# One 512-column matmul over high and low activations per high weight tile in the first MLP product, with four PSUM banks a group

## The chip, the core and the metric

The kernel runs on one core of a Trainium2 chip. Its time is device time in microseconds (us), the median over executions. A core has a matrix engine (TensorE, called PE in the profile, with the loading of its stationary operand listed as PEld), a vector engine (VectorE, DVE), an activation engine (ScalarE, ACT), GpSimd (POOL) and a queue for transfers from and to HBM (SP). PE writes its products into PSUM, eight banks of 128 partitions by 512 fp32 values. DVE and ACT read PSUM and SBUF; each engine runs its own instructions in a fixed order and waits for the others by semaphores.

## What is computed

Two layers of a post-norm trunk over 256 tokens of 2048 channels. The part of a layer that the change touches is the MLP, a product with 2048x8192 weights, a squared ReLU, and a product back:

```python
    mix = jnp.concatenate([attn, h], axis=-1) @ w_out
    x = layer_norm(ALPHA * x + mix, ln1_g, ln1_b)

    f = jnp.square(jax.nn.relu(x @ w1)) @ w2
    return layer_norm(ALPHA * x + f, ln2_g, ln2_b)
```

Ahead of the MLP stand an input projection, attention over 8 heads, a depthwise convolution and an output projection.

## The kernel before

**Products.** Everything is fp32 and has to keep most of that precision. Each operand of a large product is held as two parts in a matmul format (type fp32r in the rows): a high part, rounded, and a low part, the remainder. A product is three passes: high weights by high activations, high weights by low activations, low weights by high activations, all summed in PSUM. The activations after a LayerNorm lie as tiles `xTa` (channels on partitions, columns 0 to 255 the high part of 256 tokens, columns 256 to 511 the low part).

**Weights.** They come in chunks of 1 MB (128 partitions by 2048 columns), in the order of use that `chunk_order` (L165) lists. `load_next` (L206) issues the transfer on SP; `cutting` (L220) rounds the chunk to `wh` on ACT (L236) and subtracts it to `wl` on DVE (L237, recorded as L86 like all that goes through the counting helper), each in two pieces. `get` keeps three chunks cut ahead of use. All chunks, raw or cut, and the squared activations `h` lie in 20 slots of SBUF, handed out first in, first out (`big`, `drop`, L130).

**The MLP of a layer.** The 8192 hidden channels are 16 groups of 512. Group 0 (`mlp_first`, L1018) has the activations stationary, since it starts while the LayerNorm still hands over tiles. Groups 1 to 15 (`mlp_in`, L1038) have the weights stationary: for each of the 4 chunks `kc` of a group, each of its 4 row blocks `ki` and each of 4 column blocks `m`, `stat_w` (L294) issues three matmuls of 256 columns, high by high, high by low, low by high, into the same half of a bank; two banks hold a group. That is 30 calls in both layers, 30 x 64 = 1920 triples, 5760 matmuls. At a group's end, per bank: ACT makes the ReLU from PSUM (`rl`, L1051), DVE multiplies PSUM's positive part by it (`sq`), ACT rounds that into `h` (L143), DVE subtracts for the low part. After groups 1 to 3 the second product (`w2`, tiles `w` in the rows) takes four groups at a time, with 512-column matmuls: in(4), product 0, in(5) to in(7), in(8), product 1 and so on; the last product goes through `close` (L653), which also starts the next LayerNorm.

**PSUM.** Four banks (tag `mm`, L115) serve the products, three (`ax`) the turning of tiles and small results, one (`cv0`) the convolution.

**Order.** The order of instructions on each engine comes from a scheduler that simulates a timeline of the whole program; it isn't written out by hand. A change in one part can move neighbours elsewhere.

Of the kernel before, what the change touches and what calls it, by code (L numbers as in the profile page):

```python
# [8 lines left out]
F32 = mybir.dt.float32  # L9
# [28 lines left out]
LEAD = 3.0  # L38
# chunks of weights whose low parts GpSimd computes: columns u by (group, rows), output projection by (columns, rows)
POOL_U = ((2, 3), (3, 0))  # L40
POOL_O = ((0, 0), (0, 1), (1, 0), (1, 1), (2, 0), (2, 1), (3, 1))
POOL_LO = {("u", 0, 0, kc) for kc in range(4)} | {("u", l, i, kc) for l in range(L) for i, kc in POOL_U} | {
    ("wo", l, 0, n, kc) for l in range(L) for n, kc in POOL_O}
# tiles (tokens, channels) of the input that VectorE gives their gain and offset
GV = ((1, 0), (1, 1), (0, 2))
# [24 lines left out]
def hybrid_trunk(ctx: ExitStack, tc: tile.TileContext, x, positions, inv_freq, ln_in_g, ln_in_b,  # L70
# [5 lines left out]
    class Counted:  # L76
        """an engine whose instructions add their rough cost to the clock, for the order in which work is issued."""
        def __init__(self, eng, key, cost):
# [32 lines left out]
    sm = ctx.enter_context(tc.tile_pool(name="sm", bufs=4))  # L111
    pp = ctx.enter_context(tc.tile_pool(name="pp", bufs=4, space=bass.MemoryType.PSUM))

# [1 line left out]
    def psum(name):  # L115
        return pp.tile([P, 512], F32, name=name, tag="mm", bufs=4)

    def psumx(name):
        return pp.tile([P, 512], F32, name=name, tag="ax", bufs=3)

    def psumc(name):
        return pp.tile([P, 512], F32, name=name, tag="cv0", bufs=1)

# [20 lines left out]

# [1 line left out]
    def rows(w, k0, nk):  # L146
# [122 lines left out]

# [1 line left out]
    vconv = []  # L271
# [20 lines left out]

# [1 line left out]
    def stat_w(ps, hi, lo, ki, ncol, act, first, last):  # L294
        """ps[m//2][:, m%2] += W[:, m]^T act, the weights stationary; act holds hi | lo."""
        for m in range(ncol // P):
            o = v3(ps[m // 2], 2)[:, m % 2]
            c = slice(m * P, (m + 1) * P)
            tensor.matmul(o, lhsT=hi[:, ki, c], rhs=act[:, 0:S], start=first and m % 2 == 0, stop=False,
                             skip_group_check=True)  # L300
            tensor.matmul(o, lhsT=hi[:, ki, c], rhs=act[:, S:2 * S], start=False, stop=False,
                             skip_group_check=True)
            tensor.matmul(o, lhsT=lo[:, ki, c], rhs=act[:, 0:S], start=False, stop=last,
                             skip_group_check=True)

    def stat_x(o, hi, lo, ki, act, t, first, last):
        """o += act[:, t]^T W, the activations stationary."""
        xh = act[:, t * P:(t + 1) * P]
        xl = act[:, S + t * P:S + (t + 1) * P]
        tensor.matmul(o, lhsT=xh, rhs=hi[:, ki], start=first, stop=False)  # L310
        tensor.matmul(o, lhsT=xh, rhs=lo[:, ki], start=False, stop=False)
        tensor.matmul(o, lhsT=xl, rhs=hi[:, ki], start=False, stop=last)

# [1 line left out]
    X = cst.tile([P, 2, D], F32, name="X")  # L315
# [80 lines left out]
    def after_norm(N, keys, ps, lag):  # L396
        """the first product after a LayerNorm, activations stationary: token tile 0 leads by lag chunks."""
        def mm(t, kc):
# [34 lines left out]

# [1 line left out]
    class First(Norm):  # L435
        """the input's LayerNorm: gain and offset per partition after the turn, over the free axis later."""
        def nrm(self, t, n, eng=None):
# [80 lines left out]
    def prepare():  # L518
        """small parameters with channels on partitions; rope tables with tokens on partitions."""
        wdr = big("wdr")  # L520
# [53 lines left out]
    def rope(dst, src, t, nh, name):  # L574
        """dst (P, nh, 64) SBUF from src (P, nh, 64) PSUM."""
        c = cosT[:, t].unsqueeze(1).unsqueeze(1).broadcast_to([P, nh, 2, 32])
        s = sinT[:, t].unsqueeze(1).unsqueeze(1).broadcast_to([P, nh, 2, 32])
        s4 = src.rearrange("p h (a c) -> p h a c", a=2)
        d4 = dst.rearrange("p h (a c) -> p h a c", a=2)
        a = work(f"ra{name}", "rp", 2).rearrange("p (h a c) -> p h a c", a=2, c=32)[:, :nh]  # L580
        b = work(f"rb{name}", "rp", 2).rearrange("p (h a c) -> p h a c", a=2, c=32)[:, :nh]
        vector.tensor_tensor(out=a, in0=s4, in1=c, op=ALU.mult)
        vector.tensor_tensor(out=b, in0=s4, in1=s, op=ALU.mult)
        vector.tensor_tensor(out=d4[:, :, 0], in0=a[:, :, 0], in1=b[:, :, 1], op=ALU.subtract)
        vector.tensor_tensor(out=d4[:, :, 1], in0=a[:, :, 1], in1=b[:, :, 0], op=ALU.add)

    def convolve(l, i, h, ca):
        """taps of the depthwise convolution for two channel tiles, one a step."""
        acc = [psumc(f"cv{l}{i}0")[:, :S], work(f"cv{l}{i}1", "cva1", 1, S)]
# [18 lines left out]
    def out_part(ps, tag, l, k0, n, kc, act, last):  # L608
        """PSUM of both token tiles += act^T W over chunk kc of the rows from k0, columns of chunk n."""
        hi, lo = get(tag, l, k0, n, kc)  # L610
# [7 lines left out]
    def out_tail(ps, tag, l, k0, n, act, tail, between):  # L618
        """the same for the last chunks, token tile 0 first."""
        nch = len(act)  # L620
# [32 lines left out]
    def close(tag, l, k0, act, N, first=False):  # L653
        """the last addition to X over all column chunks, the LayerNorm starting with token tile 0."""
        def between(i, ps):
# [19 lines left out]
    for l in range(L):  # L675
        hg = v3(big(f"hg{l}"), 8)
        ca = v3(big(f"ca{l}"), 8)

# [1 line left out]
        if l == 0:  # L680
# [25 lines left out]

# [1 line left out]
        gqb = work(f"gq{l}", "gb", 2)  # L708
# [46 lines left out]
        nc.gpsimd.memset(qrk[:, 1024:1024 + 2 * S], 0.0)  # L755
# [1 line left out]
        def u_group(i):  # L757
# [18 lines left out]

# [1 line left out]
        state.update(ahead=2, cap=5)  # L778
# [24 lines left out]

# [1 line left out]
        qn = v3(big(f"qn{l}"), H)  # L805
# [66 lines left out]

# [1 line left out]
        mixT = []  # L874
# [68 lines left out]

# [1 line left out]

        def cuts_after(i0, i1, ins):
            """the chunks of the output projection's second half from i0 are cut after these instructions."""
            first = index["wo", l, 8, 0, 0]
            for i in range(first + i0, first + i1):
                cut_after[i] = ins  # L950
# [39 lines left out]

# [1 line left out]
        ps2 = [out_banks("wo", l, 0, n) for n in range(2)]  # L992
# [21 lines left out]

# [1 line left out]
        hT = {}  # L1016
# [21 lines left out]
        def mlp_in(g):  # L1038
            ps = [psum(f"f{l}{g}{j}") for j in range(2)]
            for kc in range(4):  # L1040
                hi, lo = get("w1", l, g, kc)
                for ki in range(4):
                    stat_w(ps, hi, lo, ki, 512, N.xT[kc][:, ki], kc == 0 and ki == 0, kc == 3 and ki == 3)
                    if ki == 3:
                        retire("w1", l, g, kc)
                    tick()
            h = v3(big(f"h{l}_{g}", F32R), 4)
            hT[g] = h
            for j in range(2):
                r = work(f"rl{l}{g}{j}", "ev", 4)  # L1050
                nc.scalar.activation(r, ps[j], AF.Relu)  # L1051
                q = work(f"sq{l}{g}{j}", "ev", 4)
                vector.scalar_tensor_tensor(out=q, in0=ps[j], scalar=0.0, in1=r, op0=ALU.max, op1=ALU.mult)
                split(h[:, 2 * j:2 * j + 2, 0:S], h[:, 2 * j:2 * j + 2, S:2 * S], v3(q, 2))

        mlp_first(0)
        for g in range(1, QG):
            mlp_in(g)
        for q in range(NG // QG):
# [10 lines left out]
            else:  # L1070
                N.release()
                N = Norm(f"b{l}", ln2_g[l], ln2_b[l], last=l == L - 1)
                N.load()
                close("w2", l, q * 16, act, N)
                drop(*[f"h{l}_{q * QG + i}" for i in range(QG)])
# [34 lines left out]
```

## Time and profile before

| | |
|---|---|
| time, median of 3 runs (lowest to highest) | 2090.47 us (2089.58 to 2090.71) |
| span of the profiled execution | 2086.6 us |
| PE busy in it | 2013.5 us (97%), 12438 matmuls |
| DVE busy | 1316.8 us (63%), 1706 instructions |
| ACT busy | 896.8 us (43%), 1175 instructions |
| POOL busy | 211.4 us (10%) |
| mean granted clock of TensorE | 0.988 |

The span goes from the first to the last instruction. The two layers follow each other: layer 0's MLP lies between about 328 and 1055 us of the span, layer 1's between about 1346 and 2075. A busy share is a mean over stages with different limits, so the rows further down are by stage. In names such as f<-xTa,wh the tile before the arrow is written, the others are read.

### The profile page before, as it was taken

What the parts mean: (1) busy time and instruction counts of PE and PEld (TensorE: products, weight loads), DVE (VectorE), ACT (ScalarE), POOL (GpSimd) and SP (SyncE); (2) the same over time, 40 slices, a digit from 0 to 9 for tenths busy, and PEclk for the clock granted to TensorE, in tenths of its full rate; (3) what the DMA queues carried; (4) which work ended last, traced back from release to release, by engine and by line L of the source; (5) the groups of instructions that cost most, each with busy time, mean ns of one, the idle gap of its engine ahead of it and who ended that gap; (6) DMA issues with size and microseconds to landing.
All of it is one profiled execution on the core that took longest, in us unless ns stands there. A gap on an engine that the chain in (4) does not pass through costs nothing. (4 is left out here: it accounts for less than half of the span.)

```text
span 2086.6 us, 29734 instructions
## 1 busy us (share of the span) xinstructions
PE 2013.5 (97%) x12438; PEld 1815.8 (87%) x12438; DVE 1316.8 (63%) x1706; ACT 896.8 (43%) x1175; POOL 211.4 (10%) x152
## 2 busy tenths in 40 slices
PE   6899899999999999999999988999999999999997
PEld 5798787998998899899879987789889989988986
DVE  5999987545555545455569998865455455545455
ACT  5445464443443434344345544553334434434341
POOL 6412312000000000000020133110000000000001
PEclk9899999999999999999999999999999999999999
DMA  8465264545645655566546535544565456456561
GB/s 252 135 189 171 101 242 149 194 163 201 214 151 195 208 162 188 196 222 210 173 164 177 156 124 201 179 163 162 183 221 182 162 199 212 154 191 212 189 227 68
DMA packets 225317, 377.89 MB, mean 181 GB/s; under 512 B 15858, under 2 KB 69986, under 8 KB 223904
## 3 DMA queue, kind: packets, MB, share of 16 engines
q1 hardware_dynamic: 225120, 375.99, 54.1%
q8 instruction: 97, 1.59, 0.3%
q14 instruction: 36, 0.29, 0.0%
q10 hardware_dynamic: 64, 0.02, 0.0%
HBM read 373.88 MB, written 2.10 MB: 180 GB/s over the span
## 5 line engine op out<-in xcount | busy, mean ns | idle before, releaser
L86 DVE TENSOR_TENSOR wl<-wr,wh 128x1024 fp32r<-128x1024 f32 (+1 forms) x648 | 771.3, 1229 | 566.7 <-ACT wh L236 337.7
L236 ACT CAST wh<-wr 128x1024 fp32r<-128x1024 f32 (+2 forms) x700 | 685.7, 1031 | 809.8 <-DVE wl L86 353.1
L86 PE MATMUL f<-xTa,wh 128*128 128x256 f32 x3840 | 692.5, 283 | 0.0
L86 PE MATMUL w<-wh,h 128*128 128x512 f32 x2048 | 631.9, 389 | 0.0
L86 PEld LDWEIGHTS f<-xTa,wh 128*128 128x128 f32 x3840 | 599.4, 192 | 0.7
L86 PE MATMUL f<-xTa,wl 128*128 128x256 f32 x1920 | 542.8, 283 | 3.3 <-DVE wl L86 3.3
L86 PEld LDWEIGHTS w<-wh,h 128*128 128x128 f32 x2048 | 384.4, 188 | 79.7
L86 PE MATMUL w<-wl,h 128*128 128x512 f32 x1024 | 398.4, 389 | 0.0
L86 PEld LDWEIGHTS f<-xTa,wl 128*128 128x128 f32 x1920 | 368.2, 192 | 3.8 <-DVE wl L86 3.7
L86 DVE SCALAR_TENSOR_TENSOR cv<-hg,wdT,cv 128x255 f32<-128x255 f32 (+21 forms) x480 | 248.8, 576 | 4.3 <-ACT cv L592 4.1
L86 PEld LDWEIGHTS w<-wl,h 128*128 128x128 f32 x1024 | 192.2, 188 | 39.6
L323 POOL TENSOR_TENSOR rb<-vb,mhalf 128x1 f32<-128x1 f32 x4 | 4.2, 1047 | 1413.1 <-DVE nmub L86 1413.1
L237 POOL TENSOR_TENSOR wl<-wr,wh 128x1024 fp32r<-128x1024 f32 (+1 forms) x52 | 114.0, 2217 | 224.2 <-ACT wh L236 110.9
L86 PE MATMUL wo<-wh,mx 128*128 128x512 f32 x256 | 88.3, 421 | 11.8 <-DVE mx L86 10.9
L86 PE MATMUL wo<-wh,mc 128*128 128x512 f32 x256 | 79.9, 391 | 0.0
L86 DVE TENSOR_TENSOR X<-X,w 128x512 f32<-128x512 f32 x48 | 32.8, 687 | 72.7 <-PE w L86 72.6
L86 PE MATMUL u<-xTi,wh 128*128 128x256 f32 x384 | 73.8, 293 | 0.0
L86 PE MATMUL u<-xTb,wh 128*128 128x256 f32 x384 | 72.2, 289 | 0.0
L86 PEld LDWEIGHTS wo<-wh,mx 128*128 128x128 f32 x256 | 50.7, 200 | 23.8 <-DVE mx L86 12.1
L86 DVE SCALAR_TENSOR_TENSOR sq<-f,rl 128x512 f32<-128x512 f32 x64 | 42.6, 684 | 36.0 <-ACT rl L1051 33.0
L1051 ACT ACTIVATE rl<-f 128x512 f32<-128x512 f32 x60 | 34.8, 593 | 67.6 <-PE f L86 66.8
L86 PEld LDWEIGHTS u<-xTi,wh 128*128 128x128 f32 x384 | 63.0, 200 | 0.2
(218 smaller groups left out, 1746.3 us busy)
## 6 DMA issues: line engine op xcount, KB each, us to landing
wr<-in_w_dram SPq DMA_DIRECT2D x256, 1024.0 KB, 5.1
wr<-in_w_out_dram SPq DMA_DIRECT2D x32, 1024.0 KB, 5.8
wr<-in_w_in_dram SPq DMA_DIRECT2D x60, 512.0 KB, 5.0
wr<-in_w_in_dram SPq DMA_DIRECT2D x8, 1024.0 KB, 7.3
wr<-in_w_uq_dram SPq DMA_DIRECT2D x24, 256.0 KB, 4.6
wr<-in_w_in_dram SPq DMA_DIRECT2D x8, 640.0 KB
wr<-in_w_ukv_dram SPq DMA_DIRECT2D x8, 512.0 KB, 4.3
X<-in_x_dram SPq DMA_DIRECT2D x8, 256.0 KB, 3.9
```

Source lines behind the costliest of these rows:

```text
L86: return f(*args, **kw)
L236: nc.scalar.copy(hi[:, c], raw[:, c])
L237: eng.tensor_sub(lo[:, c], raw[:, c], hi[:, c].bitcast(F32))
L323: nc.gpsimd.tensor_tensor(out=r, in0=v, in1=mhalf, op=ALU.pow)
L1051: nc.scalar.activation(r, ps[j], AF.Relu)
```

## The change

`stat_w2` issues, for each triple, one 512-column matmul of the high weights over `xTa`'s high and low halves together, into a whole bank, and one 256-column matmul of the low weights over the high half, into the bank's first half. A group therefore needs four banks instead of two. They are taken in two pairs, `b` = 0 (column blocks 0, 1) and `b` = 1 (blocks 2, 3); the loops go `kc`, `b`, `ki`, and the pair `b` = 0 is read out in the middle of the last chunk. To read a bank out, ACT copies its second half (128x256) to SBUF and DVE adds the first half to it; ReLU, square and split follow on SBUF, per pair as before. The ring of product banks becomes six from the end of group 0 to the last product: `lend` moves one bank of `ax` and the convolution's into it and back. `h`'s slot is taken at a group's start instead of its end. The rest of the diff only takes comments out and gives each bank its own tag.

```diff
-    pp = ctx.enter_context(tc.tile_pool(name="pp", bufs=4, space=bass.MemoryType.PSUM))
...
+    pp = ctx.enter_context(tc.tile_pool(name="pp", bufs=1, space=bass.MemoryType.PSUM))
...
+    banks = dict(mm=[0, 1, 2, 3], ax=[4, 5, 6], cv=[7])
+
+    def bank(name, ring):
+        i = banks[ring].pop(0)
+        banks[ring].append(i)
+        return pp.tile([P, 512], F32, name=name, tag=f"b{i}")
...
+    def lend(to, *moves):
+
+        for ring, i in moves:
+            banks[ring].remove(i)
+        banks[to][:0] = [i for _, i in moves]
...
+    def stat_w2(o, hi, lo, ki, m, act, first, last):
+
+
+        c = slice(m * P, (m + 1) * P)
+        tensor.matmul(o, lhsT=hi[:, ki, c], rhs=act[:, 0:2 * S], start=first, stop=False, skip_group_check=True)
+        tensor.matmul(o[:, 0:S], lhsT=lo[:, ki, c], rhs=act[:, 0:S], start=False, stop=last, skip_group_check=True)
...
         def mlp_in(g):
-            ps = [psum(f"f{l}{g}{j}") for j in range(2)]
+            ps = []
+            h = v3(big(f"h{l}_{g}", F32R), 4)
+            hT[g] = h
+
+            def squares(b):
+
+                f = work(f"f{l}{g}s{b}", "ev", 4)
+                for j in range(2):
+                    c = slice(j * S, (j + 1) * S)
+                    nc.scalar.copy(f[:, c], ps[2 * b + j][:, S:2 * S])
+                    vector.tensor_add(f[:, c], ps[2 * b + j][:, 0:S], f[:, c])
+                r = work(f"rl{l}{g}{b}", "ev", 4)
+                nc.scalar.activation(r, f, AF.Relu)
+                vector.scalar_tensor_tensor(out=f, in0=f, scalar=0.0, in1=r, op0=ALU.max, op1=ALU.mult)
+                split(h[:, 2 * b:2 * b + 2, 0:S], h[:, 2 * b:2 * b + 2, S:2 * S], v3(f, 2))
+
             for kc in range(4):
                 hi, lo = get("w1", l, g, kc)
-                for ki in range(4):
-                    stat_w(ps, hi, lo, ki, 512, N.xT[kc][:, ki], kc == 0 and ki == 0, kc == 3 and ki == 3)
-                    if ki == 3:
-                        retire("w1", l, g, kc)
-                    tick()
...
+                for b in range(2):
+                    if kc == 0:
+                        ps += [psum(f"f{l}{g}{2 * b + j}") for j in range(2)]
+                    for ki in range(4):
+                        for m in (2 * b, 2 * b + 1):
+                            stat_w2(ps[m], hi, lo, ki, m, N.xT[kc][:, ki], kc == 0 and ki == 0, kc == 3 and ki == 3)
+                        if ki % 2:
+                            if b and ki == 3:
+                                retire("w1", l, g, kc)
+                            tick()
+                    if kc == 3:
+                        squares(b)
 
         mlp_first(0)
+        lend("mm", ("ax", 6), ("cv", 7))
...
+                lend("ax", ("mm", 6))
+                lend("cv", ("mm", 7))
                 close("w2", l, q * 16, act, N)
```

Three places in the instruction order show it. In the names, f020 is layer 0, group 2, bank 0; wh53 and wl53 are the high and low part of chunk 53; xTa00 are channels 0 to 511 of the activations. "waits" names the engine whose semaphore an instruction waits for.

PE where group 2 of layer 0 starts, before:

```order
L86 MATMUL f020_3529<-xTa00_3043,wh53_3350 128x256 [waits Activation_49]
L86 MATMUL f020_3529<-xTa00_3043,wh53_3350 128x256
L86 MATMUL f020_3529<-xTa00_3043,wl53_3351 128x256
L86 MATMUL f020_3529<-xTa00_3043,wh53_3350 128x256 x2
L86 MATMUL f020_3529<-xTa00_3043,wl53_3351 128x256
L86 MATMUL f021_3530<-xTa00_3043,wh53_3350 128x256 x2
L86 MATMUL f021_3530<-xTa00_3043,wl53_3351 128x256
```

The same group on PE now, where its first pair of banks hands over to the second:

```order
L86 MATMUL f021_3485<-xTa00_3043,wh53_3337 128x512
L86 MATMUL f021_3485<-xTa00_3043,wl53_3338 128x256
L86 MATMUL f022_3502<-xTa00_3043,wh53_3337 128x512 [waits DVE_49]
L86 MATMUL f022_3502<-xTa00_3043,wl53_3338 128x256
L86 MATMUL f023_3503<-xTa00_3043,wh53_3337 128x512 [waits DVE_49]
L86 MATMUL f023_3503<-xTa00_3043,wl53_3338 128x256
```

Three matmuls of 256 columns became one of 512 and one of 256, and the first matmul into a group's third and fourth bank now waits for the DVE additions of the group before, which held these banks.

ACT around the end of group 5 of layer 0, before (`wr` is a raw chunk, DMAHW a transfer):

```order
L236 CAST wh89_5073<-wr89_5015 128x1024 [waits DMAHW1_49,DVE_49]
L236 CAST wh89_5073<-wr89_5015 128x1024
L236 CAST wh90_5129<-wr90_5071 128x1024 [waits DMAHW2_49,DVE_49]
L236 CAST wh90_5129<-wr90_5071 128x1024
L1051 ACTIVATE rl050_5001<-f050_4774 128x512 [waits PE_49]
L1051 ACTIVATE rl051_5007<-f051_4775 128x512 [waits PE_49]
L143 CAST h0_5_5000<-sq050_5003 128x2x256 [waits DVE_49]
L143 CAST h0_5_5000<-sq051_5009 128x2x256 [waits DVE_49]
```

And now:

```order
L249 CAST wh88_4746<-wr88_4683 128x1024 [waits DMAHW0_49,PE_49]
L249 CAST wh88_4746<-wr88_4683 128x1024
L1068 COPY f05s0_4707<-f050_4567 128x256 [waits PE_49]
L1068 COPY f05s0_4707<-f051_4568 128x256 [waits PE_49]
L1071 ACTIVATE rl050_4712<-f05s0_4707 128x512 [waits DVE_49]
L1068 COPY f05s1_4733<-f052_4585 128x256 [waits PE_49]
L249 CAST wh89_4790<-wr89_4744 128x1024 [waits DMAHW1_49,PE_49]
L249 CAST wh89_4790<-wr89_4744 128x1024
L1068 COPY f05s1_4733<-f053_4586 128x256 [waits PE_49]
L156 CAST h0_5_4558<-f05s0_4707 128x2x256 [waits DVE_49]
```

The read-out begins one weight chunk earlier in the row of casts, and its second pair has a chunk's casts between its two copies. DVE's row has the additions and the subtractions `wl` in the same places.

PE in the start of layer 0's MLP, before (f000 and f001 are group 0's banks for token tiles 0 and 1, the chunks of group 0 are 45 to 48, of group 1 49 to 52):

```order
L86 MATMUL f011_3291<-xTa00_3043,wh49_3197 128x256 x2
L86 MATMUL f011_3291<-xTa00_3043,wl49_3198 128x256
L86 MATMUL f010_3290<-xTa00_3043,wh49_3197 128x256 [waits Activation_49]
L86 MATMUL f010_3290<-xTa00_3043,wh49_3197 128x256
L86 MATMUL f011_3291<-xTa00_3043,wh49_3197 128x256 x2
L86 MATMUL f000_3079<-wh48_3177,xTa03_3108 128x512 [waits Activation_49]
L86 MATMUL f000_3079<-wl48_3178,xTa03_3108 128x512
L86 MATMUL f010_3290<-xTa00_3043,wl49_3198 128x256 [waits DVE_49]
```

And now:

```order
L86 MATMUL f001_3080<-wl45_2934,xTa00_3043 128x512
L86 MATMUL f001_3080<-wh45_2933,xTa00_3043 128x512
L86 MATMUL f000_3079<-wh48_3177,xTa03_3108 128x512 [waits Activation_49]
L86 MATMUL tra012_3123<-ident_82,X_70 128x128 [waits PE_49,Pool_49]
L86 MATMUL tra012_3123<-ident_82,X_70 128x128 x3
L86 MATMUL f000_3079<-wl48_3178,xTa03_3108 128x512 [waits DVE_49]
L86 MATMUL f000_3079<-wh48_3177,xTa03_3108 128x512 x2
L86 MATMUL f000_3079<-wl48_3178,xTa03_3108 128x512
L86 MATMUL f000_3079<-wh48_3177,xTa03_3108 128x512
L86 MATMUL f000_3079<-wh48_3177,xTa03_3108 128x512 [waits Activation_49]
L86 MATMUL f011_3300<-xTa00_3043,wh49_3197 128x512 [waits Activation_49]
```

Before, rows of group 1 stood ahead of f000's last chunk (wh48); now that chunk follows f001's first directly, and group 1 begins after it with banks 1 to 3, its bank 0 being the lent one that group 0 still uses.

## Rows read from the trace of the kernel before

**Rows 1.** Busy time of each engine over the whole span (share, instructions).

```profile
PE 2013.5 (97%) x12438; PEld 1815.8 (87%) x12438; DVE 1316.8 (63%) x1706; ACT 896.8 (43%) x1175; POOL 211.4 (10%) x152
```

**Rows 2.** Chain that ended last: start us, length us, what; last part.

```profile
1560.14 92.15 PE f L86 x768
1652.30 87.07 PE w L86 x384
1739.36 92.15 PE f L86 x768
1831.51 87.07 PE w L86 x384
1918.58 69.11 PE f L86 x576
```

**Rows 3.** Stretches: us, busy PE, PEld, DVE, ACT, POOL (instructions), clock, DMA share, GB/s.

```profile
328.00:380.00 52.00, 48.43 (x308) 42.68 (x307) 36.01 (x39) 29.65 (x38) 12.16 (x9) 1.00 0.50 170
380.00:1055.00 675.00, 674.47 (x4255) 614.22 (x4254) 347.04 (x345) 270.25 (x299) 3.75 (x3) 1.00 0.56 188
...
1200.00:1346.00 146.00, 133.05 (x701) 114.12 (x700) 131.79 (x226) 65.88 (x112) 37.55 (x16) 0.95 0.47 166
...
1393.00:2075.00 682.00, 681.76 (x4316) 621.45 (x4314) 346.79 (x345) 268.38 (x298) 4.57 (x3) 1.00 0.54 183
...
1560.00:1652.00 92.00, 92.00 (x768) 92.00 (x767) 45.92 (x46) 38.44 (x45) 0.00 (x0) 1.00 0.52 178
1652.00:1739.00 87.00, 87.00 (x387) 72.05 (x386) 44.31 (x43) 34.02 (x37) 0.00 (x0) 1.00 0.60 198
```

**Rows 4.** PE timeline where widths mix: start us, length us, instruction.

```profile
1377.34 0.39 PE L86 MATMUL f<-wh,xTa 128*128 128x512 f32 x1
1377.57 0.40 PE L86 MATMUL f<-xTa,wh 128*128 128x256 f32 x2
1377.80 0.28 PE L86 MATMUL f<-xTa,wl 128*128 128x256 f32 x1
```

**Rows 5.** Groups by form: line, engine, operation, count | busy us, mean ns | idle before.

```profile
L86 PE MATMUL f<-xTa,wh 128*128 128x256 f32 x3840 | 692.5, 283 | 0.0
...
L86 PEld LDWEIGHTS f<-xTa,wh 128*128 128x128 f32 x3840 | 599.4, 192 | 0.7
L86 PE MATMUL f<-xTa,wl 128*128 128x256 f32 x1920 | 542.8, 283 | 3.3 <-DVE wl L86 3.3
...
L1051 ACT ACTIVATE rl<-f 128x512 f32<-128x512 f32 x60 | 34.8, 593 | 67.6 <-PE f L86 66.8
...
L603 ACT COPY ca<-cv 128x256 f32<-128x256 f32 x16 | 6.0, 392 | 20.0 <-DVE cv L86 20.0
...
L86 DVE TENSOR_TENSOR rt<-raq,rbq 128x256 f32<-128x256 f32 x8 | 3.0, 411 | 0.0
```

**Rows 6.** ACT timeline, one group's end, with the wait before in brackets.

```profile
1582.55 2.00 ACT L236 CAST wh<-wr 128x1024 fp32r<-128x1024 f32 x2 [3.50 <-DMA wr<-in_w_dram]
1584.45 1.08 ACT L1051 ACTIVATE rl<-f 128x512 f32<-128x512 f32 x2
```

**Rows 7.** DVE timeline, the same group's end.

```profile
1583.15 2.36 DVE L86 TENSOR_TENSOR wl<-wr,wh 128x1024 fp32r<-128x1024 f32 x2 [3.40 <-issue]
1585.43 1.28 DVE L86 SCALAR_TENSOR_TENSOR sq<-f,rl 128x512 f32<-128x512 f32 x2
```

**Rows 8.** PE's waits from 1330 to 1400: us in total, times, longest.

```profile
PE f L86 <- DVE wl L86: 1.6, 1, 1.6
PE f L86 <- DVE xTa L86: 1.1, 1, 1.1
PE tra L86 <- DVE X L86: 0.6, 1, 0.6
```

**Rows 9.** ACT timeline ahead of layer 1's last product.

```profile
1984.67 2.00 ACT L236 CAST wh<-wr 128x1024 fp32r<-128x1024 f32 x2 [6.59 <-DMA wr<-in_w_dram]
```

**Rows 10.** PE's waits from 1200 to 1346, layer 1's attention.

```profile
PE pT L86 <- DVE pr L86: 6.3, 2, 4.7
PE wo L86 <- DVE mx L86: 5.9, 2, 5.2
```

More of the change, by code (lines that the diff above doesn't have):

```diff
@@ L111, in hybrid_trunk @@
     sm = ctx.enter_context(tc.tile_pool(name="sm", bufs=4))
-    pp = ctx.enter_context(tc.tile_pool(name="pp", bufs=4, space=bass.MemoryType.PSUM))
+    pp = ctx.enter_context(tc.tile_pool(name="pp", bufs=1, space=bass.MemoryType.PSUM))
[4 more added lines that the diff above has]
+        return pp.tile([P, 512], F32, name=name, tag=f"b{i}")
     def psum(name):
-        return pp.tile([P, 512], F32, name=name, tag="mm", bufs=4)
+        return bank(name, "mm")
     def psumx(name):
-        return pp.tile([P, 512], F32, name=name, tag="ax", bufs=3)
+        return bank(name, "ax")
     def psumc(name):
-        return pp.tile([P, 512], F32, name=name, tag="cv0", bufs=1)
+        return bank(name, "cv")
+    def lend(to, *moves):
+        for ring, i in moves:
+            banks[ring].remove(i)
+        banks[to][:0] = [i for _, i in moves]
     def work(name, tag, bufs, cols=512):
@@ L1038, in mlp_in @@
         def mlp_in(g):
-            ps = [psum(f"f{l}{g}{j}") for j in range(2)]
+            ps = []
[11 more added lines that the diff above has]
+                split(h[:, 2 * b:2 * b + 2, 0:S], h[:, 2 * b:2 * b + 2, S:2 * S], v3(f, 2))
             for kc in range(4):
                 hi, lo = get("w1", l, g, kc)
-                for ki in range(4):
-                    stat_w(ps, hi, lo, ki, 512, N.xT[kc][:, ki], kc == 0 and ki == 0, kc == 3 and ki == 3)
-                    if ki == 3:
-                        retire("w1", l, g, kc)
-                    tick()
[L1047 to L1054, printed above, removed]
+                for b in range(2):
[10 more added lines that the diff above has]
+                        squares(b)
         mlp_first(0)
+        lend("mm", ("ax", 6), ("cv", 7))
         for g in range(1, QG):
```

## The prediction

> **What bounds the kernel now.** I read the busy line first: PE is busy 97% of the span, DVE 63%, ACT 43% [rows 1]. That is a mean, so the stretches come next. In the two long MLP stretches PE is busy 674.47 of 675 us and 681.76 of 682 us, at a granted clock of 1.00, its upper level of 2.4 GHz [rows 3]; what one matmul takes there goes straight into the time. The chain of waits says the same: from 1560 us on it is PE alone, alternating between the first product (f, 92.15 us for 768 matmuls, four groups) and the second (w, 87.07 us for 384) [rows 2]. Beside PE, DVE is busy 45.92 and ACT 38.44 of 92 us, and DMA's share is 0.52 [rows 3]. So PE's own pace sets the time in both MLPs, about 1357 of 2086.6 us. Only in their starts, in the attention and in the last LayerNorm does another engine end last; the attention stretch of layer 1 has DVE at 131.79 of 146 us and PE at 133.05 [rows 3].
>
> **What a matmul takes.** Busy time of single matmuls (283 ns in the groups [rows 5]) counts a pipelined overlap and must not be multiplied. The pace is the chain's length over its count: 92.15/768 = 0.11999 us for 256 columns, 87.07/384 = 0.22675 us for 512 [rows 2]. The 256 columns more cost 0.10676 us, which at 2.4 GHz is the columns alone; so each matmul carries about 0.0132 us that don't depend on its width. Every matmul here has a weight load of its own (3840 and 1920 loads for as many matmuls [rows 5]), so these 13 ns are what a matmul with its load costs beyond its columns. Does the pace hold when widths alternate? In the MLP's start a 512 is followed 0.23 us later by two 256s, these by the next 0.23 us later [rows 4]: the paces add.
>
> **The gain.** A triple takes 3 x 0.11999 = 0.35997 us now and 0.22675 + 0.11999 = 0.34674 us after: 0.01323 us less. 1920 triples give 25.4 us, all on PE where PE is the chain. A stretch of four groups should go from 92.15 to 256 x 0.34674 = 88.77 us. The loads removed (1920 of 192 ns [rows 5]) already lie beside matmuls and give nothing of their own.
>
> A rule speaks against the size of this. The Trainium skill, "TensorE: Matmul & The Clock Gate", section Back-to-back issue gap, gives a warm start-to-start of N/2.4 ns plus about 2.5 ns for one isolated stream of matmuls. By that a merged pair would save 2.5 ns, as an estimate 4.8 us in all and a time near 2086. The trace doesn't agree: 120.0 and 226.7 ns stand where the rule has 109 and 216, and I keep the trace's.
>
> **What is added.** Per group four ACT copies and four DVE additions of 128x256, 120 of each. The nearest rows are a copy of that shape at 392 ns and an addition at 411 ns [rows 5]: 47 us on ACT and 49 us on DVE in all. ReLU and square (593 ns for a ReLU from PSUM [rows 5]) keep their shapes. In a stretch of four groups that is 16 x 0.411 = 6.6 us on a DVE busy 46 and 6.3 us on an ACT busy 38, beside 88.8 us of PE: hidden, as a sum. If the cover were gone it would cost up to 49 us. The same 1 MB chunks must come in 88.8 instead of 92.15 us; the second product already takes them at a chunk per 5.4 us (16 in 87.07) with a DMA share of 0.60 [rows 3], so transfers keep up.
>
> **The new wait.** The third and fourth bank of a group are those of the group before's first pair. From that pair's last matmul to their next use PE has the second pair's last chunk and the first pair's first chunk of the next group: 8 + 8 triples, 5.55 us. There are 22 such hand-overs (groups that follow one another directly, 11 a layer); elsewhere 87 us of second product lie between. Both engines work in order, so behind what do the copies stand? ACT has a chunk's casts ahead of them (2.00 us), DVE its subtractions (2.36 us) [rows 6, 7]. These can be cast while the last chunk runs, because their slots came free before it. Bounds from below: two copies and the last addition, 2 x 0.392 + 0.411 = 1.2 us. From above: a cast pair, the copies, a subtraction pair and an addition one after another, 2.00 + 0.78 + 2.36 + 0.41 = 5.55 us, just the room. Before, such a read-out began 1.27 us after the group's end (1560.14 + 92.15/4 = 1583.18 to 1584.45) and ended 3.5 us after it [rows 2, 6, 7]; that is the nearest case. I take 0. Behind a waiting copy stand later casts, and behind these the weights; PE's lack of any wait in the stretches shows that they have reserve. `h`'s slot, taken a group earlier, leaves the weights one slot less for some 22 us: 0 too.
>
> **Before the last product** the first bank is used again at the group's end, 2.77 us after its last matmul; 25 matmuls into it (5.7 us) go ahead of the second bank. Here a cast once waited 6.59 us for its transfer, ending 3 us ahead of the group's end at 1987.69 [rows 2, 9], and the second copy now stands behind that cast. Bounds 0 to 2 us a layer; I take 0, since in this row the transfer came in time.
>
> **The MLP's start.** PE waits there 1.6 + 1.1 + 0.6 us [rows 8], layer 0 the same; the stretch has 48.43 of 52 us busy [rows 3]. The new order loses group 1's rows as filler ahead of f000's last chunk (28 matmuls of 256, 3.4 us) and runs them right after it instead; turns of X stand earlier in the row and make up for part of that. Either the wait on wl shrinks (1.6 us a layer, most of which shows again at the next chunk, so -1), or up to 2 us of the lost filler show as waiting: -2 to +4 us for both layers. I take +1, the middle. In the attention, which PE enters with another ring state, the scheduler reorders neighbours; PE waits 6.3 and 5.9 us there for DVE [rows 10], and half of the smaller either way bounds it: -3 to +3, I take 0. POOL and the SP queue get no new work; two transfers of a layer swap places.
>
> **Sum.** Span 2086.6 - 25.4 + 1 = 2062.2 us. The profiled execution is 3.9 us shorter in span than the median time; with that 2066 us. The unknowns alone reach 5 down and 10 up (start 3, attention 3, last product 4): 2061 to 2076.
>
> **Rivals.**
> *A, the small losses come:* start +4, last product +4, attention +3: about 2076. Inside the range, as forecast otherwise.
> *B, slower: the read-out misses its room.* A copy that stands behind a cast which waits for a transfer (6.59 us once [rows 9]) is late by that wait, and PE stops at each hand-over. The gain left is 25.4 - 1 = 24.4 us, so it decides from 24.4/22 = 1.1 us past the room, that is a read-out of 6.7 us. With 2 us past at each, 44 us: 2066 + 44 = 2110. For it: the order puts casts between the copies. Against it: the first two copies stand together, only the second pair's are parted, and that pair has a whole group until its banks are used; the 3.5 us above.
> *C, the gain doesn't come:* the 13 ns go with each 256 columns of activations, not with each matmul, and a wide one over high and low halves keeps them. Then a pair takes 0.360 us and the time is 2066 + 25 = 2091. For it: in the 512-column matmuls of the trace, which carry them once [rows 2], the moving operand is weights, not high and low activations. Against it: both are 512 neighbouring columns of one tile.
>
> **How the numbers follow.** About 0.2% (4 us) is what a measurement of this kernel can tell from no change. Forecast with A 92 in 100, B 4, C 4. B's time lies above 2094.7, C's within 0.2% of 2090.5, all of the forecast below 2086.3. So faster 0.92, same 0.04, slower 0.04. The range: 2060 (one below the lower end, as the pace is rounded) to 2076, leaving out B and C and some of both tails.
>
> **What would show it.** In the trace after: a stretch of four groups of 88.8 us, with 512 and 256 starting 0.227 and 0.120 us apart (gain right); 92 us would be C. Waits of PE for DVE at a group's first matmul into its third bank, 22 of them of microseconds: B. DVE about 52 and ACT about 45 us in such a stretch: the added work as costed. MLP starts of 52 and 47 us by the same rows, and the attention's 146, within 3 us: the rest right. Wrong would be a pace that isn't the sum of the two, or weights that come late because the first-in-first-out rows have tightened.

## The result, and the profile of the changed kernel

The changed kernel takes 2070.72 us (median of 4, 2069.61 to 2071.32) against 2090.02 us for the kernel before, a ratio of 0.9909 (95% interval 0.9897 to 0.9921). It is 19.3 us faster; 24.4 were forecast, and the time lies within the range of 2060 to 2076. The profiled execution has a span of 2068.4 us, 18.2 less than before. The direction and the range held; the way there did not. The merging itself gave about 15 us instead of 25.4, and the MLP's start gave 4.5 us where the forecast had put a loss of 1.

The busy line, which answers to [rows 1]:

```profile
PE 1999.6 (97%) x10518; PEld 1712.9 (83%) x10518; DVE 1359.2 (66%) x1826; ACT 935.3 (45%) x1295; POOL 210.0 (10%) x152
```

1920 matmuls and 1920 loads are gone, 120 instructions each came to DVE and ACT (42 and 39 us more busy time, 49 and 47 forecast), and PE is still the engine that is busy nearly all the time. The chain of the last part (start us, length us, what), to be laid beside [rows 2]:

```profile
1381.18 78.29 PE f L86 x445
1459.47 87.10 PE w L86 x384
1546.58 90.44 PE f L86 x512
1637.02 87.06 PE w L86 x384
1724.08 90.44 PE f L86 x512
```

A stretch of four groups went from 92.15 to 90.44 us, where 88.77 was forecast. With 256 pairs in it, a pair takes 353.3 ns and not 346.7. The second product has kept its 87.1. Stretches of the changed kernel (us, busy PE, PEld, DVE, ACT, POOL, clock, DMA share, GB/s), as in [rows 3]:

```profile
380.00:1055.00 675.00, 673.38 (x3381) 570.35 (x3380) 375.90 (x416) 295.90 (x368) 6.62 (x5) 1.00 0.58 190
1547.00:1637.00 90.00, 90.00 (x511) 78.12 (x510) 50.83 (x60) 44.83 (x61) 0.00 (x0) 1.00 0.56 180
```

PE is busy in all of the 90 us, at a granted clock of 1.00, and waits for nothing; so the missing 1.7 us per stretch lie between matmuls that follow one another, not in a wait. DVE's 50.83 and ACT's 44.83 us hold the added work, 4.9 and 6.4 us above the 45.92 and 38.44 of [rows 3] (6.6 and 6.3 were costed for a whole stretch).

A sum by sections shows the rest. Each section runs from one first or last instruction on PE to the next (the w sections end with their last matmul); all in us of the profiled executions, one of each kernel.

| section | before | changed | difference |
|---|---|---|---|
| start of the span to layer 0's first f | 330.06 | 332.08 | +2.02 |
| layer 0, first f to first w (MLP start, groups 0 to 4) | 121.85 | 116.27 | -5.58 |
| layer 0, first w to last w (groups 5 to 15) | 601.86 | 597.15 | -4.71 |
| to layer 1's first f | 297.28 | 296.32 | -0.96 |
| layer 1, MLP start | 121.86 | 117.49 | -4.37 |
| layer 1, first w to last w | 601.85 | 597.16 | -4.69 |
| last LayerNorm | 11.8 | 11.9 | +0.1 |

In the long sections 704 pairs gain 4.7 us, 6.7 ns each, half of what was forecast. The starts gain far more than their pairs' share.

Two places of PE's timeline in the changed kernel (start us, length us, instruction) show that a pair has two spacings. First group 2 of layer 0:

```profile
401.90 0.39 PE L86 MATMUL f<-xTa,wh 128*128 128x512 f32 x1
402.13 0.28 PE L86 MATMUL f<-xTa,wl 128*128 128x256 f32 x1
402.25 0.39 PE L86 MATMUL f<-xTa,wh 128*128 128x512 f32 x1
402.48 0.28 PE L86 MATMUL f<-xTa,wl 128*128 128x256 f32 x1
402.59 0.39 PE L86 MATMUL f<-xTa,wh 128*128 128x512 f32 x1
```

then group 5 of layer 1:

```profile
1547.10 0.40 PE L86 MATMUL f<-xTa,wh 128*128 128x512 f32 x1
1547.34 0.28 PE L86 MATMUL f<-xTa,wl 128*128 128x256 f32 x1
1547.46 0.40 PE L86 MATMUL f<-xTa,wh 128*128 128x512 f32 x1
1547.70 0.28 PE L86 MATMUL f<-xTa,wl 128*128 128x256 f32 x1
1547.81 0.40 PE L86 MATMUL f<-xTa,wh 128*128 128x512 f32 x1
```

The two 512s and two 256s take 0.69 us in the first, 0.71 in the second: the step from a 512 to its 256 is 0.23 or 0.24 us. Over 10 us windows the mean is 346.7 ns in layer 0 from 380 to 450 us (groups 2 to 4), and about 353 in all of its later groups; in layer 1 the rows that alternate without a break take about 347 until 1396 us, then 353. In group 2 there the scheduler put two high or two low matmuls side by side in some places, and the step is at one of them. So the forecast pace exists, and the kernel runs most of the product at another.

### The profile page after: what moved, and what is told of

Same layout as the page of the kernel before. It is cut to its first block, busy times and chain, and to the rows that moved or that the text cites. A ratio compares the mean times of both kernels' runs of the same rounds, so it can differ in the third digit from the quotient of the medians.

```text
span 2068.4 us, 26102 instructions
## 1 busy us (share of the span) xinstructions
PE 1999.6 (97%) x10518; PEld 1712.9 (83%) x10518; DVE 1359.2 (66%) x1826; ACT 935.3 (45%) x1295; POOL 210.0 (10%) x152
## 5 line engine op out<-in xcount | busy, mean ns | idle before, releaser
L86 PE MATMUL f<-xTa,wh 128*128 128x512 f32 x1920 | 676.8, 397 | 0.0
L86 PEld LDWEIGHTS f<-xTa,wh 128*128 128x128 f32 x1920 | 360.4, 188 | 87.6
L86 PEld LDWEIGHTS f<-xTa,wl 128*128 128x128 f32 x1920 | 362.7, 189 | 0.9
L86 DVE SCALAR_TENSOR_TENSOR cv<-hg,wdT,cv 128x255 f32<-128x255 f32 (+21 forms) x480 | 240.1, 557 | 5.3 <-ACT cv L612 5.1
L86 PE MATMUL wo<-wh,mx 128*128 128x512 f32 x256 | 87.1, 413 | 6.4 <-DVE mx L86 5.4
L86 PEld LDWEIGHTS u<-xTb,wh 128*128 128x128 f32 x384 | 60.8, 194 | 0.2
L86 PE MATMUL u<-xTi,wl 128*128 128x256 f32 x192 | 56.5, 294 | 0.0
```

Source lines behind the costliest of these rows:

```text
L86: return f(*args, **kw)
```

## The experiments

Two questions were open: what makes a pair 6.7 ns dearer than the sum of its two matmuls, and where the start's gain comes from. The theories on the first: (1) each change of width costs 3.3 ns; (2) the low matmul pays for following its own high one into the same bank; (3) the alternation of 512 and 256 can run at either of two spacings, chosen by what ran just ahead, and then keeps it. All kernels below are the changed kernel with the edit shown.

**Order of high and low, three ways.** Two high, two low:

```diff
                     for ki in range(4):
-                        for m in (2 * b, 2 * b + 1):
-                            stat_w2(ps[m], hi, lo, ki, m, N.xT[kc][:, ki], kc == 0 and ki == 0, kc == 3 and ki == 3)
+                        for part in (0, 1):
+                            for m in (2 * b, 2 * b + 1):
+                                stat_w2(ps[m], hi, lo, ki, m, N.xT[kc][:, ki], kc == 0 and ki == 0,
+                                        kc == 3 and ki == 3, part)
```

> Two high matmuls (512 columns, two banks), then the two low ones (256), instead of high, low, high, low; all else as in the changed kernel, where a pair takes 353.3 ns in most of the first product against the forecast 346.7. If each change of width costs 3.3 ns (half as many changes here), a pair takes 350.0 ns, four groups 89.6 us, and the kernel about 2064.5 us (6.3 us less than 2070.7). If the price is that the low matmul follows its own high one into the same bank, no low matmul does so any more: 346.7 ns, 88.8 us, about 2058.5 us. If pairs simply fall into one of two spacings by what ran before, 346.7 or 353.3 ns with jumps between them.

(`part` 0 issues the high matmul alone, 1 the low one.) Eight and eight (the loop over `part` stands outside that over `ki`):

> Eight high matmuls (four row blocks by two banks), then the eight low ones: one change of width per eight matmuls. By changes of width at 3.3 ns: 347.5 ns a pair, four groups 89.0 us, about 2059.5 us. By the same bank: 346.7 ns, 88.8 us, about 2058.5 us. By two spacings that are kept: since no single 256 stands between two 512s, only the uniform paces remain, 226.7 and 120.0 ns, together 346.7, whatever ran before.

The low matmul one pair late:

```diff
+                    steps = [(ki, m) for ki in range(4) for m in (2 * b, 2 * b + 1)]
+                    for i in range(9):
+                        for j, part in ((i, 0), (i - 1, 1)):
+                            if 0 <= j < 8:
+                                ki, m = steps[j]
+                                stat_w2(ps[m], hi, lo, ki, m, N.xT[kc][:, ki], kc == 0 and ki == 0,
+                                        kc == 3 and ki == 3, part)
```

> High and low still alternate, but the low matmul is that of the other bank's pair before, so it never follows its own high one; at the edges of a chunk's half two high or two low stand together. By changes of width: 14 of 16 changes remain, 352.5 ns a pair, four groups 90.2 us, about 2069 us. By the same bank after a high matmul: 346.7 ns, 88.8 us, about 2058.5 us. By two spacings that are kept: 353.3 or 346.7 ns, perhaps changing at the doubled matmuls.

Two and two: 2066.23 us (ratio to before 0.989, 0.9875 to 0.9904), four groups 89.16 us, 348.3 ns a pair. Eight and eight: 2066.72 us (0.989, 0.9876 to 0.9905), 89.36 us, 349.1 ns. One pair late: 2073.09 us in one run, 90.22 us, 352.4 ns. From the chains of the first two:

```profile
1543.59 89.16 PE f L86 x512
```

```profile
1543.43 89.36 PE f L86 x512
```

Theory 2 falls: in none of the three does the low matmul follow its own high one, and the third keeps nearly the whole price. Theory 1 fits the third (352.5) but not the other two: with an eighth of the changes, eight and eight should have been the cheapest at 347.5 ns, and it is dearer than two and two. What was expected by theory 3 missed as well: 346.7 for eight and eight, and one of its two spacings for two and two. The starts in the trace (kept there in whole ns), from each matmul's start to the next one's (L a 512, n a 256), say why:

```
changed, from 1560 us     L236 n113 L233 n117 L241 n120   and again: 1060 for three pairs
changed, from 420 us      L230 n117 L230 n116 L230 n117   1040 for three pairs
two and two               n112 L233 L231 n113 n119 L233 L236 n116   1393 for four pairs
eight and eight           L233 L236 L228 L233 L231 L226 L227 L227 n113 n119 n120 n120 n120 n120 n120 n120   2793 for eight pairs
```

A 512 behind 256s is not at its own pace of 227 at once: five of them pass, 26 ns in all, before it is; the first 256 behind 512s takes 113 ns, 7 less than its own pace, and the next ones 119 and 120. A change of width has no fixed price. What a matmul costs depends on several before it, and the alternation of single matmuls doesn't settle: it repeats a pattern, in the changed kernel mostly one of the two in the first lines. Theory 3 is left for it, and was not yet tested.

These three kernels also have a wait that the changed one hasn't. PE's wait at the start of layer 1's last product in two and two, from 1895 to 1975 us:

```profile
PE w L86 <- DVE f115s L86: 1.5, 1, 1.5
```

It is 1.3 us in eight and eight and 1.2 in the third, in layer 0 nearly the same, so 2.5 to 3 us of each of their times are not the pace's.

**All but the merging.** Three matmuls of 256 columns, with four banks, ring of six and the new read-out:

```diff
-        tensor.matmul(o, lhsT=hi[:, ki, c], rhs=act[:, 0:2 * S], start=first, stop=False, skip_group_check=True)
+        tensor.matmul(o[:, 0:S], lhsT=hi[:, ki, c], rhs=act[:, 0:S], start=first, stop=False, skip_group_check=True)
+        tensor.matmul(o[:, S:2 * S], lhsT=hi[:, ki, c], rhs=act[:, S:2 * S], start=False, stop=False,
+                      skip_group_check=True)
```

> Everything of the change but the merging: four banks a group, ring of six, read-out by copy and addition, yet three matmuls of 256 columns per triple. A triple should take 360 ns as before, four groups 92.2 us. The rest of the ledger shows alone: against the kernel before, the changed one was 3.9 and 2.7 us shorter in the two MLP starts beyond the pace and 2.0 us longer ahead of layer 0's MLP. If these come with the banks and the order, this kernel takes 2090.0 - 6.6 + 1 = about 2084.5 us; if they come with the merging (fewer and other matmuls as filler), about 2090 us. If the added read-out or the bank waits cost PE anything, waits of f for DVE appear and it is slower than 2090 us.

2084.83 us, ratio 0.9977 (0.9967 to 0.9986): 4.7 us faster than before with not one matmul less. Four groups take the old 92.15 us; the two MLP starts take 119.67 and 119.59 us, 2.2 less than before each. From its chain:

```profile
1557.38 92.15 PE f L86 x768
```

Against this kernel, from which the changed one differs by the merging alone, the changed one gains 3.40 us in layer 0's start (as much as 256 pairs at 13.3 ns, the full forecast, though the first pairs of group 1 run at 353), 4.71, 2.10 and 4.69 us in the other sections: 14.9 us of 25.4; by the two ratios to the kernel before it is 14.2. Beside PE's pace the read-out costs nothing that shows: PE's only waits for DVE in the first product are those of its start.

**The ring of six alone.** The old `mlp_in`, two banks a group, with `lend`:

```diff
-            ps = []
...
+            ps = [psum(f"f{l}{g}{j}") for j in range(2)]
...
+                    stat_w(ps, hi, lo, ki, 512, N.xT[kc][:, ki], kc == 0 and ki == 0, kc == 3 and ki == 3)
```

> The kernel before with the ring of six banks alone: three matmuls of 256 columns, two banks a group, read-out from PSUM as before. Four groups take 92.2 us. With everything but the merging, each MLP start (first f to first w) was 2.2 us shorter than before (119.6 against 121.85 us). If the larger ring brings that, by letting the scheduler place group 1 elsewhere, the starts here take about 119.6 us and the kernel 2085 us; if the four banks a group or the read-out in halves bring it, the starts take 121.9 us and the kernel about 2089.5 us.

2085.03 us, ratio 0.9979 (0.997 to 0.9988); the starts take 119.60 and 119.62 us. So the ring alone is enough for the whole gain of the starts. PE's waits from 1320 to 1400 us in this kernel, as in the changed one:

```profile
PE f L86 <- DVE xTa L86: 1.1, 1, 1.1
PE tra L86 <- DVE X L86: 0.6, 1, 0.6
```

Of [rows 8] the wait of f for wl (1.6 us) is gone, and one of 0.2 us for ACT besides. PE's timeline of the kernel before shows the place:

```profile
1366.56 0.72 PE L86 MATMUL f<-xTa,wh 128*128 128x256 f32 x4
1368.91 0.39 PE L86 MATMUL f<-xTa,wl 128*128 128x256 f32 x1 [1.63 <-DVE wl L86]
```

There group 1 started early as filler, behind 48 of group 0's 96 matmuls, and its first low matmul stood in PE's row when that chunk's low part was not cut yet, with the rest of group 0 queued behind it. With the ring of six, group 1's first matmul comes behind 55 of them and its first low one behind 62, and it doesn't wait. The rest of the 2.2 us, some 0.35, isn't traced to a place.

**What sets the spacing.** The first high matmul of some groups in pieces, all else untouched:

```diff
+        k = 2 if part else 1
+        w = 2 * S // k
+        for i in range(k):
+            tensor.matmul(o[:, i * w:(i + 1) * w], lhsT=hi[:, ki, c], rhs=act[:, i * w:(i + 1) * w],
+                          start=first and i == 0, stop=False, skip_group_check=True)
```

Two pieces of 256 in every group:

> As the changed kernel, but the first high matmul of each of the 30 groups goes as two of 256 columns. That alone adds 30 x 13.3 ns = 0.4 us. If alternating pairs keep one of two spacings, chosen by what ran just before, the other start into each group can change the spacing of the whole group: 346.7 ns throughout would be four groups of 88.8 us and about 2060.5 us, 353.3 throughout 90.5 us and about 2071 us; jumps between the two at group boundaries also belong to this theory. If the spacing has a lasting cause (addresses, DVE and ACT beside it, the weight supply), nothing but the 0.4 us changes: the first groups of layer 0 at 346.7, all after the first second product at 353.3, about 2071 us.

Four of 128 (`k` = 4) in groups 1, 5, 9 and 13 of each layer:

> As the changed kernel, but the first high matmul of groups 1, 5, 9, 13 (the first after the start or after a second product) goes as four of 128 columns; this costs up to 0.3 us each, 2.4 us in all. In the changed kernel four 128-column transposes stood just ahead of the stretches that ran at 346.7 ns. If the spacing is set by what ran before, these four should set it too: 88.8 us per four groups and about 2062 us. If not: 90.7 us and about 2072 us.

Two pieces: 2071.35 us (0.9912, 0.9897 to 0.9927), four groups 90.47 us:

```profile
1547.72 90.47 PE f L86 x516
```

Four pieces: **2062.55 us** (0.9869, 0.9852 to 0.9885). Its chain and its timeline where layer 1's second product ends and group 5 begins:

```profile
1543.78 88.97 PE f L86 x515
1632.76 87.08 PE w L86 x384
```

```profile
1543.39 0.39 PE L86 MATMUL w<-wh,h 128*128 128x512 f32 x1
1543.62 0.56 PE L86 MATMUL f<-xTa,wh 128*128 128x128 f32 x4
1544.02 0.33 PE L86 MATMUL f<-xTa,wl 128*128 128x256 f32 x1
1544.18 0.40 PE L86 MATMUL f<-xTa,wh 128*128 128x512 f32 x1
1544.42 0.28 PE L86 MATMUL f<-xTa,wl 128*128 128x256 f32 x1
1544.54 0.40 PE L86 MATMUL f<-xTa,wh 128*128 128x512 f32 x1
1544.77 0.28 PE L86 MATMUL f<-xTa,wl 128*128 128x256 f32 x1
1544.89 0.39 PE L86 MATMUL f<-xTa,wh 128*128 128x512 f32 x1
1545.12 0.28 PE L86 MATMUL f<-xTa,wl 128*128 128x256 f32 x1
1545.23 0.39 PE L86 MATMUL f<-xTa,wh 128*128 128x512 f32 x1
```

Four short matmuls ahead, two pairs of 0.36 and 0.35 us, and from then on 0.23 and 0.12 us without a change: 346.7 ns in every 10 us window of all six stretches behind a second product, up to 255 pairs after one altered instruction. This is theory 3, shown for these stretches: from each layer's first second product to its last, the rows of PE, DVE and ACT stand in the same order, by names and shapes, as in the changed kernel, but for the three high matmuls in pieces, so the spacing can't come from the addresses, the weight supply or DVE and ACT beside PE alone. In layer 1's first groups the pieces didn't help: from the doubled matmuls of group 2 on, the pace was 353 as in the changed kernel. The two pieces of 256 did nothing there, and in layer 0's first groups, which ran at 346.7 in the changed kernel, the pace was 353.

The same pieces in the middle of stretches, in groups 3, 7, 11 and 15, and once more at the starts with group 2 added:

> The four 128-column pieces at the first high matmul of groups 3, 7, 11, 15 instead of 1, 5, 9, 13. If they set the spacing that the alternation then keeps, groups 5 and 6 after a second product run at 353.3 ns a pair and 7 and 8 at 346.7, 9 and 10 at 353.3, 11 and 12 at 346.7, 13 and 14 at 353.3, 15 at 346.7: the step sits where the pieces are. Four groups 2 x 22.6 + 2 x 22.2 + 0.2 = 89.9 us, the kernel about 2066.5 us. If the earlier kernel's spacing came from something else (another order, other addresses), the step is not at these groups: 88.9 or 90.7 us for four.

> Pieces at groups 1, 5, 9, 13 and at group 2 besides, since layer 1's groups 2 to 4 still ran at 353.3 ns (lost where the scheduler put two high matmuls side by side in group 2). If the pieces set the spacing wherever they stand, layer 1's stretch from 1400 us on runs at 346.7 too, unless the doubled matmuls come behind them: 1.2 us less for 0.4 us of pieces, about 2061.7 us against 2062.6; the difference lies inside what the times can tell, the pace in the trace shows it.

The first took 2072.04 us in one run, four groups 90.64 us; its expectation failed. Groups 7 and 8, 11 and 12 and 15 stayed at 353, in layer 1 group 3 went from 353 to 346.7 as expected, in layer 0 the pieces turned 346.7 into 353. The second took 2063.79 us (0.9875, 0.9859 to 0.9892), the same as without group 2 within what the times tell. At the added pieces both layers went from 346.7 to 353. In layer 1 that lasted for 4 us: at the doubled matmuls, with which the changed kernel goes to 353, this one came back to 346.7 at about 1396 us, and groups 3 and 4 ran at it. So the pieces set the good spacing behind a steady row of 512s (all 12 places with that setting, in two kernels); inside an alternation pieces and doubled matmuls change it, or not, and why wasn't resolved.

**Without the lent banks.**

```diff
-        lend("mm", ("ax", 6), ("cv", 7))
...
-                lend("ax", ("mm", 6))
-                lend("cv", ("mm", 7))
```

> The changed kernel without the lending: a group takes all four banks, so its first pair of banks is that of the group before it at once, and the read-out has the second pair's last chunk to run in, 2.8 us, in place of 5.5. The copies and additions of a pair take some 1.2 us when nothing stands ahead of them on ACT and DVE, up to 5.5 us behind a chunk's casts and subtractions. If they run unhindered, PE loses nothing: about 2071 us. If casts stand ahead of them, PE waits for DVE at the 22 hand-overs, 1 to 3 us each, 22 to 66 us: 2093 to 2137 us, the forecast's slower rival made real. The scheduler can soften it by working one bank after the other.

2065.41 us (2 runs; 0.9883, 0.9864 to 0.9903): neither of the two outcomes that were written down, but 5 us faster than the changed kernel. PE has no wait of f for DVE in it except those of the start, so the smaller room is enough in the order that this kernel has; for the changed kernel's own order that isn't shown. The scheduler now puts doubled 512s and 256s at each change of groups, and in the stretches behind a second product the spacing flips at them: 353 in the first group, about 347 in the next two, 353 in the last; four groups take 89.64 us. Its MLP starts take 117.0 and 117.2 us, close to the changed kernel's, with group 1 behind 55 and 62 of group 0's matmuls again: four banks a group without the lent ones move the filler too. That it is faster is the pace: 2.3 us in each of the long sections.

## Why the prediction was right and where not

**What bounds the kernel** held: PE's own pace, in both MLPs, before and after.

**The gain** is the step that failed, in its last question, whether the pace holds when widths alternate. The prediction answered it from [rows 4], where one 512 stands ahead of a row of 256s, so that no alternation is in it, and the rows print starts in steps of 10 ns. A pair's two spacings differ by 6.7 ns. The sum of 226.7 and 120.0 is right for one of them, met in groups 2 to 4 of layer 0 and in layer 1 up to the first pairs of group 2; the others run at 353.3. So the term is 14.9 us and not 25.4; with the four pieces in place 8.2 of the missing 10.5 us come back (2062.55 against 2070.72). The prediction did name "a pace that isn't the sum of the two" as what would make it wrong, but gave it no price and no rival.

The rule of the Trainium skill ("TensorE: Matmul & The Clock Gate", section Back-to-back issue gap) that would have made the gain 4.8 us is not borne out: at the good spacing a pair takes 346.7 ns where it has 325, and there taking a matmul away gives 13.3 ns. The same section of the Trainium skill says that in a real kernel the spacing is set by weight loads and matmuls together, in a pipeline; no run here takes the two apart, and the 131 ns that it gives for 512 columns are far from the 226.7 here.

**The MLP's start** was put at -2 to +4 us, +1 taken; it is -4.5 us. The prediction saw that group 1 lost its place as filler and that the wait on wl might go, but thought most of it would show again at the next chunk. It didn't: the filler was itself what waited. This miss, 5.5 us, hid half of the gain's.

**The added work** was sized right (a copy takes 372 ns and an addition 420 in the trace, 392 and 411 taken; DVE 50.83 and ACT 44.83 us of 90 against 52 and 45 of 88.8) and hidden. **The new wait** is 0, as taken. The first read-out of group 5 in layer 1 on ACT, then on DVE (its pair of banks is full at about 1566.4):

```profile
1563.44 2.00 ACT L249 CAST wh<-wr 128x1024 fp32r<-128x1024 f32 x2 [8.84 <-PE f L86]
1566.03 0.72 ACT L1068 COPY f15s<-f 128x256 f32<-128x256 f32 x2 [0.59 <-PE f L86]
```

```profile
1564.52 2.36 DVE L86 TENSOR_TENSOR wl<-wr,wh 128x1024 fp32r<-128x1024 f32 x2 [4.32 <-ACT wh L249]
1566.80 0.75 DVE L86 TENSOR_TENSOR f15s<-f,f15s 128x256 f32<-128x256 f32 x2
```

The casts are done before the banks are full, ACT waits for PE, and the last addition ends at 1567.55, 1.2 us after: the lower bound. Rival B's wait didn't come up at any hand-over, nor in the kernel without the lent banks. **The last product** lost nothing (87.06 us), but the risk was real: the 1.2 to 1.5 us a layer in the three kernels of another order lie in the 0 to 2 that were its bounds. **Rival A**'s small losses didn't come: start, last product and the stretch ahead of layer 1's MLP stand at -4.5, 0 and -1.0. **Rival C** is out: with the good spacing the merged matmul carries the 13 ns once.

**The stages ahead**: +2.0 us before layer 0's MLP, -1.0 before layer 1's. Over all kernels of this document the first lies between 330.1 and 332.7 us for nearly the same work, and no run here says what makes the difference.

That the size came out near the forecast is in part luck: a term 10 us too large and one 5 us too low stood against each other. Without the second the time would have been about 2076, at the range's upper end. The range itself has a slip: start and attention, 3 us each, reach 6 us down and not 5; its lower end of 2060 covers that.

## What to carry to other kernels

A pace read from uniform rows isn't the pace of a mixture: before costing a mixed stream, find a place in the trace where the same mixture runs for long, and work in mean spacing over many, not in single steps of the timeline. If a stream on PE runs slower than its parts and nothing is waited for, look at whether its spacing is constant over the whole run; where it jumps, an instruction at the start may be worth more than any in the loop. And filler work that stands ahead of a late operand on an in-order engine can cost more than the gap it fills.

## What the runs showed of the hardware

- Alternating matmuls of 512 and 256 columns, each with its own weight load, run at one of two mean spacings, 346.7 or 353.3 ns a pair, at the same granted clock of 1.00, and keep it for up to 255 pairs here. Behind a steady row of 512s they took the longer one (six places of the changed kernel); with four 128-column matmuls between, the shorter (12 of 12). Two of a width side by side inside the alternation could change it either way: to 353 in layer 1 of the changed kernel, to 347 in the one without the lent banks.
- In rows of eight and eight, a 512 after 256s needs about five of its kind to come back to 226.7 ns, 26 ns in all; after 512s the first 256 takes 113 ns. Uniform rows had 226.7 ns in the second product of all kernels, and 120.0 ns in the first product of the three that keep 256 columns.
- What makes the two spacings, and why pieces inside an alternation change it in some places and not in others, stays open.
